# Four-layer hybrid model on one Trainium2 core: activations as the loaded operand, weights streamed 512 columns wide

## The chip, the cores and the metric

One program on one core of a Trainium2 chip. The metric is the time of one execution in microseconds of device time; lower is better. Three executions of the kernel before are listed, and one further execution was taken by the hardware profiler. The engines are named as the profile names them: PE is TensorE's matrix multiplications and PEld its loads of the stationary operand, DVE is VectorE, ACT is ScalarE, POOL is GpSimd, and SP is the engine whose queue issues most of the transfers.

## The reference: what is computed

256 tokens of 1024 features go through four layers. Each layer is a half-weighted SwiGLU feed-forward network (FFN), a mixer, and a second FFN, each on an RMS-normed input and added to the residual x. The mixers are S5, HGRN2, a gated delta net (GDN) and MoBA attention, one per layer. A last RMS norm gives the output.

```python
def _swiglu(x, w_gate, w_up, w_down):
    return (jax.nn.silu(x @ w_gate) * (x @ w_up)) @ w_down
...
    for i in range(DEPTH):
        m, j = i % N_MIXERS, i // N_MIXERS
        x = x + 0.5 * _swiglu(_rms(x, norm_g[i, 0]), ffn_w_gate[i, 0], ffn_w_up[i, 0], ffn_w_down[i, 0])
        h = _rms(x, norm_g[i, 1])
...
        x = x + y.astype(x.dtype)
        x = x + 0.5 * _swiglu(_rms(x, norm_g[i, 2]), ffn_w_gate[i, 1], ffn_w_up[i, 1], ffn_w_down[i, 1])
    return _rms(x, final_norm_g)
```

The inner width of an FFN is 2816, so an FFN multiplies by two matrices of 1024 x 2816 and one of 2816 x 1024, all in 32-bit floats. There are eight FFNs; they hold most of the weights.

## The kernel before, in words

Every product is split in three. A weight tile is cut into a high part (`hi`, a rounding copy on ScalarE, L73) and a low part (`lo`, the difference, on VectorE, L76), and the activations are cut likewise. `mm3` (L310 to L316) then issues high x high, high x low and low x high into one PSUM sum. All of them use the type float32r.

```python
        t.matmul(p, hi, ah, start=first, stop=False)
        t.matmul(p, hi, al, start=False, stop=False)
        t.matmul(p, lo, ah, start=False, stop=last)
```

The first operand of `matmul` is loaded into the array, 128 x 128, and the second streams through it. So in `mm3` the weights are loaded and the activations stream: x is kept turned, as `self.x` [128 features, 8, 256 tokens], with its split copies `self.xh` and `self.xl`, and a product streams 256 columns, the tokens. `col_tile` (L346) makes one tile of 128 output features x 256 tokens from 24 such products for 8 tiles of the contraction. Only `proj_rows` (L389, the v and gate projections of the mixers) loads x and streams weights, 256 columns wide (L400 to L402).

The class `Weights` plans all weights of the program in the order of use. A block is a transfer of up to 1 MB on SP's queue, four of them are held (`RAW`); a unit is 128 x 1024 elements, eight tiles of the contraction x 128 features, and four units are held in split form (`HL`). `take` hands out a unit and `pump` starts the loads and the splits that have become possible. Each unit feeds 24 products.

`ffn` (L414) goes over 22 tiles of the inner width. For each it makes the gate's and the up projection's tile, and `evac` (L420) makes the inner activations: a product with the norm's factors on VectorE (`a`), Silu on ScalarE (`sl`), a product with the up tile on VectorE (`h`), and the split (`hh` on ScalarE, `hl` on VectorE). The result already lies as the next products want it, with features on the partitions. `residual` (L452) makes the eight tiles of the down projection; each is scaled by the norm's factors (`part`), added to x and handed to `done_x` (L206), which splits it for the next part (`xh`, `xl`), squares it on ScalarE (`sq`) and sums the squares on GpSimd (`sqsum`). At the start of a part `norm_col` (L266) and `norm_due` (L275) make the norm's factors with small products on TensorE.

Beside the first FFN run the preparations of S5 (`s5_prep`, L602), spread over the FFN's steps. The bias table of MoBA (`moba_bias`, L1733) is asked for after the second FFN's inner loop; a DMA on ScalarE's queue copies it to DRAM (`bias_rows`, L1750). The order on each engine is not the order of the code: a scheduler places the instructions by its own estimate of when their operands are there, except where the code pins them. Within an engine the order is then fixed, and an instruction that waits holds all behind it.

## Time and profile before

| what | value |
|---|---|
| three executions, median (lowest to highest) | 2305.3 us (2305.07 to 2307.87) |
| the profiled execution: its span (no other time of it is listed) | 2303.2 us |
| TensorE products / weight loads | busy 2184.3 us (95%) / 2128.4 us (92%), 18575 each |
| VectorE, ScalarE, GpSimd | busy 1612.2 us (70%), 1152.3 us (50%), 362.7 us (16%) |
| DMA | 390.02 MB, mean 169 GB/s |

A busy TensorE is not one at its peak: the ends of its products are modelled and overlap, so its pace is read from the distance of one start to the next. A part's limit is read in its own stretch, since the eight FFNs and the four mixers have different ones.

### The profile page before, as it was taken

What the parts mean: (1) busy time and instruction counts of PE and PEld (TensorE: products, weight loads), DVE (VectorE), ACT (ScalarE), POOL (GpSimd) and SP (SyncE); (2) the same over time, 40 slices, a digit from 0 to 9 for tenths busy, and PEclk for the clock granted to TensorE, in tenths of its full rate; (3) what the DMA queues carried; (4) which work ended last, traced back from release to release, by engine and by line L of the source; (5) the groups of instructions that cost most, each with busy time, mean ns of one, the idle gap of its engine ahead of it and who ended that gap; (6) DMA issues with size and microseconds to landing.
All of it is one profiled execution on the core that took longest, in us unless ns stands there. A gap on an engine that the chain in (4) does not pass through costs nothing.

```text
span 2303.2 us, 44828 instructions
## 1 busy us (share of the span) xinstructions
PE 2184.3 (95%) x18575; PEld 2128.4 (92%) x18575; DVE 1612.2 (70%) x2712; ACT 1152.3 (50%) x1920; POOL 362.7 (16%) x380
## 2 busy tenths in 40 slices
PE   8979887999999999999999888889999999999998
PEld 7978677999999999999999777789999999999998
DVE  7998655666666877666667788877666666666664
ACT  5544334444445755444444476664544444455443
POOL 1499620001001000001001333222000000001001
PEclk9999888999999999999999999999999999999999
DMA  8656956655556535546555433224555555645553
GB/s 232 191 165 223 246 117 192 190 168 192 183 179 195 178 120 186 187 159 193 183 179 184 150 102 101 75 84 146 181 185 180 173 188 186 208 153 167 187 163 101
DMA packets 380572, 390.02 MB, mean 169 GB/s; under 512 B 11392, under 2 KB 374080, under 8 KB 379344
## 3 DMA queue, kind: packets, MB, share of 16 engines
q1 hardware_dynamic: 377520, 383.91, 53.1%
q10 hardware_dynamic: 2656, 3.16, 0.8%
q8 instruction: 145, 2.38, 0.4%
q0 software_dynamic: 192, 0.10, 0.1%
q14 instruction: 59, 0.48, 0.1%
HBM read 375.12 MB, written 12.01 MB: 168 GB/s over the span
## 4 chain that ended last, share of the span: by engine, by line
PE 78%; DVE 9%; ACT 3%; POOL 3%; DMA 3%; issue 3%; SPq 0%; ACTq 0%; DVEq 0%; POOLq 0%
PE acc L315 24%; PE acc L314 23%; PE acc L316 23%; DVE lo L76 2%; DMA tab<-s_k 1%; DVE cy L1422 1%; DMA raw<-in_s_w_glu_dram 1%; PE acc L401 1%; PE acc L400 1%; PE acc L402 1%; ACT hi L73 1%; DVE xl L221 0%; POOL s5e L742 0%; POOL s5e L743 0%; ACT zb L1546 0%
## 5 line engine op out<-in xcount | busy, mean ns | idle before, releaser
L76 DVE TENSOR_TENSOR lo<-raw,hi 128x1024 fp32r<-128x1024 f32 (+1 forms) x664 | 816.6, 1231 | 379.8 <-ACT hi L73 372.3
L73 ACT CAST hi<-raw 128x1024 fp32r<-128x1024 f32 (+1 forms) x697 | 714.6, 1028 | 665.9 <-PE acc L315 447.3
L315 PE MATMUL acc<-xl,hi 128*128 128x256 f32 x3336 | 946.8, 284 | 3.3 <-DVE xl L221 3.2
L314 PE MATMUL acc<-xh,hi 128*128 128x256 f32 x3336 | 946.6, 284 | 2.0 <-ACT xh L220 1.4
L316 PE MATMUL acc<-xh,lo 128*128 128x256 f32 x3336 | 944.6, 283 | 0.9 <-DVE lo L76 0.9
L315 PEld LDWEIGHTS acc<-xl,hi 128*128 128x128 f32 x3336 | 635.5, 191 | 6.1 <-DVE xl L221 5.3
L314 PEld LDWEIGHTS acc<-xh,hi 128*128 128x128 f32 x3336 | 634.7, 190 | 5.9 <-issue 2.3
L316 PEld LDWEIGHTS acc<-xh,lo 128*128 128x128 f32 x3336 | 635.0, 190 | 1.9 <-DVE lo L76 1.2
L314 PE MATMUL acc<-hh,hi 128*128 128x256 f32 x1408 | 401.1, 285 | 5.5 <-ACT hi L73 5.5
L316 PE MATMUL acc<-hh,lo 128*128 128x256 f32 x1408 | 400.1, 284 | 0.6 <-DVE lo L76 0.6
L315 PE MATMUL acc<-hl,hi 128*128 128x256 f32 x1408 | 400.2, 284 | 0.0
L314 PEld LDWEIGHTS acc<-hh,hi 128*128 128x128 f32 x1408 | 269.2, 191 | 6.3 <-ACT hi L73 5.7
L316 PEld LDWEIGHTS acc<-hh,lo 128*128 128x128 f32 x1408 | 268.6, 191 | 0.9 <-DVE lo L76 0.9
L315 PEld LDWEIGHTS acc<-hl,hi 128*128 128x128 f32 x1408 | 268.7, 191 | 0.4 <-issue 0.4
L238 POOL TENSOR_TENSOR sqsum<-sq 128x256 f32<-128x256 f32 x13 | 14.4, 1110 | 1120.7 <-ACT sq L230 1120.7
L427 ACT CAST hh<-h 128x256 fp32r<-128x256 f32 x176 | 71.1, 406 | 204.3 <-DVE h L426 204.1
L428 DVE TENSOR_TENSOR hl<-h,hh 128x256 fp32r<-128x256 f32 x176 | 77.5, 442 | 69.5 <-ACT hh L427 69.5
L422 DVE TENSOR_TENSOR a<-acc,r_row 128x256 f32<-128x256 f32 x176 | 74.4, 423 | 69.3 <-PE acc L316 69.1
L238 POOL TENSOR_TENSOR sqsum<-sqsum,sq 128x256 f32<-128x256 f32 x65 | 63.6, 978 | 304.5 <-ACT sq L230 292.4
L76 POOL TENSOR_TENSOR lo<-raw,hi 128x1024 fp32r<-128x1024 f32 x33 | 82.3, 2495 | 179.3 <-ACT hi L73 166.0
L424 ACT ACTIVATE sl<-a 128x256 f32<-128x256 f32 x176 | 72.6, 413 | 45.9 <-DVE a L422 45.6
L400 PE MATMUL acc<-hi,xh 128*128 128x256 f32 x320 | 93.2, 291 | 0.0
(576 smaller groups left out, 2669.6 us busy)
## 6 DMA issues: line engine op xcount, KB each, us to landing
raw<-in_ffn_w_gate_dram SPq DMA_DIRECT2D x87, 1024.0 KB, 5.4
raw<-in_ffn_w_up_dram SPq DMA_DIRECT2D x87, 1024.0 KB, 5.8
raw<-in_ffn_w_down_dram SPq DMA_DIRECT2D x64, 1024.0 KB, 5.4
raw<-in_ffn_w_down_dram SPq DMA_DIRECT2D x32, 768.0 KB, 4.7
raw<-in_gdn_w_in_dram SPq DMA_DIRECT2D x24, 1024.0 KB, 5.5
raw<-in_hg_w_in_dram SPq DMA_DIRECT2D x16, 1024.0 KB, 5.4
raw<-in_moba_w_in_dram SPq DMA_DIRECT2D x12, 1024.0 KB, 5.3
raw<-in_s_w_glu_dram SPq DMA_DIRECT2D x8, 1024.0 KB, 8.5
```

Source lines behind the costliest of these rows:

```text
L73: pin(self.nc.scalar.copy(hi, src))
L76: eng.tensor_tensor(lo, src, hi.bitcast(F32), op=OP.subtract)
L238: eng.tensor_tensor(s, self.sq[0], sq, op=OP.add)
L314: t.matmul(p, hi, ah, start=first, stop=False)
L315: t.matmul(p, hi, al, start=False, stop=False)
L316: t.matmul(p, lo, ah, start=False, stop=last)
L400: self.nc.tensor.matmul(p[:, t], xh, hi[:, k % 4], start=k == 0, stop=False)
L401: self.nc.tensor.matmul(p[:, t], xl, hi[:, k % 4], start=False, stop=False)
L422: nc.vector.tensor_tensor(a, p[:, 0], self.r_row, op=OP.mult)
L424: nc.scalar.activation(sl, a, AF.Silu)
L427: nc.scalar.copy(hh[:, f], h)
L428: return nc.vector.tensor_tensor(hl[:, f], h, hh[:, f].bitcast(F32), op=OP.subtract)
```

## The change

The two operands change places in nearly all products. The activations become the loaded operand, 128 features x 128 tokens, and the weights stream, 512 columns wide; one product now does the work of two. x lies as rows of tokens, `self.x` [128 tokens, 2, 1024]. A unit of weights is now two tiles of the contraction x 512 columns, and feeds twelve products (`Model.wide`): three for each tile of the contraction and each half of the tokens. For the FFN's inner layer the 512 columns are 256 of the gate and 256 of the up matrix, brought by two transfers into one block. The q and k projections and the like (`proj_cols`) stay as they were.

What follows from the turned layout:

- An output tile is now [128 tokens, 512 features], so the FFN's inner activations have to be turned before the down projection: `turn` transposes four tiles of 128 x 128 on TensorE per 256 inner features, one unit's products behind, and the split follows from PSUM in tiles of 128 x 512.
- The norm's factor is a scalar per partition and goes into Silu and into the last scale; the instructions `a` and `part` are gone.
- `turn_x` transposes each finished 128 x 512 piece of x on TensorE and splits it from PSUM. Squares are summed by ScalarE's accumulator; GpSimd's sums, and the small products of the norm on TensorE, go (they stay in the three mixers that still use the row `r_row`).
- The last units of a product (`tail`) are taken together, so that the first half of the tokens ends early and is turned while the second half is multiplied; the first product of a part starts with that first half.
- The final output needs no transposes.

```diff
-    def block(self, w, k0, nk, c0, ncol, units):
+    def wide(self, srcs, k0, nk, first=False):
+        step = 2 if first else 4
+        for k in range(k0, k0 + nk, step):
+            n = min(step, k0 + nk - k)
+            self.units += self.block(srcs, k, n, [(u, 2, 0, 512) for u in range(0, n, 2)])
...
+    def wide(self, p, unit, a, k, t, first, last):
+        hi, lo = unit
+        mm = self.nc.tensor.matmul
+        n = hi.shape[1]
+        for j in range(n):
+            ah, al = [a[:, k + j, m, t * 128:t * 128 + 128] for m in range(2)]
+            mm(p, ah, hi[:, j], start=first and j == 0, stop=False)
+            mm(p, ah, lo[:, j], start=False, stop=False)
+            mm(p, al, hi[:, j], start=False, stop=last and j == n - 1)
+
+    def product(self, a, n, done, tail=0, step=None, ps=None, k0=0, opens=True, closes=True):
+        if ps is None:
+            ps = [self.acc.tile([128, 512], F32, name="acc") for _ in range(2)]
+        u = 0
+        while u < n:
+            m = tail if n - u == tail else 1
+            units = self.w.take(m)
+            for t in range(2):
+                for j, unit in enumerate(units):
+                    self.wide(ps[t], unit, a, k0 + 2 * (u + j), t, opens and u + j == 0, closes and u + j == n - 1)
+                if u + m == n and done is not None:
+                    done(t, ps[t])
+            u += m
...
-            a = w.block(g, 0, KT, c, 256, [(0, KT, 0, 128), (0, KT, 128, 128)])
-            b = w.block(u, 0, KT, c, 256, [(0, KT, 0, 128), (0, KT, 128, 128)])
+            w.wide([(g, c, 256), (u, c, 256)], 0, KT, not w.blocks)
...
-            def evac(f, p):
-                a = two.tile([128, L], F32, name="a")
-                nc.vector.tensor_tensor(a, p[:, 0], self.r_row, op=OP.mult)
-                sl = two.tile([128, L], F32, name="sl")
-                nc.scalar.activation(sl, a, AF.Silu)
-                h = two.tile([128, L], F32, name="h")
-                nc.vector.tensor_tensor(h, p[:, 1], sl, op=OP.mult)
-                nc.scalar.copy(hh[:, f], h)
-                return nc.vector.tensor_tensor(hl[:, f], h, hh[:, f].bitcast(F32), op=OP.subtract)
+            def evac(j, t, p):
+                sl = two.tile([128, 256], F32, name="sl", bufs=1)
+                nc.scalar.activation(sl, p[:, :256], AF.Silu, scale=self.r_col[:, t:t + 1])
+                if t == 0:
+                    waiting.append((j, two.tile([128, 2, 256], F32, name="h", bufs=1)))
+                return nc.vector.tensor_tensor(waiting[-1][1][:, t], p[:, 256:], sl, op=OP.mult)
+            def turn():
+                j, h = waiting.pop(0)
+                q = self.aux.tile([128, 512], F32, name="aux")
+                for f in range(2):
+                    for t in range(2):
+                        c = f * 256 + t * 128
+                        nc.tensor.transpose(q[:, c:c + 128], h[:, t, f * 128:f * 128 + 128], self.ident)
+                q = q.rearrange("p (f c) -> p f c", f=2)
+                hh = hhl[:, 2 * j:2 * j + 2, 0]
+                nc.scalar.copy(hh, q)
+                return nc.vector.tensor_tensor(hhl[:, 2 * j:2 * j + 2, 1], q, hh.bitcast(F32), op=OP.subtract)
...
+    def turn_x(self, t, c):
+        q = self.aux.tile([128, 512], F32, name="aux")
+        for j in range(4):
+            k = 4 * c + j
+            nc.tensor.transpose(q[:, j * 128:j * 128 + 128], self.x[:, t, k * 128:k * 128 + 128], self.ident)
...
+                nc.scalar.activation(self.xh[:, k, tok], p, AF.Copy, scale=g)
+                nc.vector.scalar_tensor_tensor(self.xl[:, k, tok], p, g, self.xh[:, k, tok].bitcast(F32),
+                                               op0=OP.mult, op1=OP.subtract)
```

In the built programs 14784 products of 256 columns become 7392 of 512, and 1560 of 256 stay. The FFNs' inner layers add 352 transposes of 128 x 128, the turning of x adds 192, of which 16 replace those that turned the input before.

How the order moved, at three places. VectorE, near the end of a gate and up loop of an FFN; `hhl` is the split of the turned inner activations, `xhl` that of the turned x. Before:

```order
L76 TENSOR_TENSOR lo<-raw,hi 128x768
L422 TENSOR_TENSOR a<-acc,r_row 128x256
L76 TENSOR_TENSOR lo<-raw,hi 128x1024
L426 TENSOR_TENSOR h<-acc,sl 128x256
L428 TENSOR_TENSOR hl<-h,hh 128x256
```

and with the change:

```order
L430 TENSOR_TENSOR h<-acc,sl 128x256 x2
L91 TENSOR_TENSOR lo<-raw,hi 128x1024 x2
L443 TENSOR_TENSOR hhl<-aux,hhl 128x2x256
L91 TENSOR_TENSOR lo<-raw,hi 128x1024 x9
L484 SCALAR_TENSOR_TENSOR x<-acc,half,x 128x512 x2
L91 TENSOR_TENSOR lo<-raw,hi 128x1024
L241 SCALAR_TENSOR_TENSOR xhl<-aux,gains,xhl 128x128 x5
```

Both halves' `h` now stand ahead of the next two splits of weights, and the split of the turned activations comes two splits of weights later; `a` and the split without a transpose are gone.

TensorE, where one part's finished x meets the products around it. Before, at the start of an FFN's products, with the norm's small products between:

```order
L315 MATMUL acc<-xl,hi 128x256
L316 MATMUL acc<-xh,lo 128x256
L270 MATMUL aux<-mean_col,sqsum 128x1 x2
L314 MATMUL acc<-xh,hi 128x256
L315 MATMUL acc<-xl,hi 128x256
```

and with the change, in the middle of a down projection, with the transposes (L230) of both halves of x's first 512 features:

```order
L348 MATMUL acc<-lo,hhl 128x512
L230 MATMUL aux<-ident,x 128x128 x4
L349 MATMUL acc<-hi,hhl 128x512
L230 MATMUL aux<-ident,x 128x128 x4
L347 MATMUL acc<-hi,hhl 128x512
```

The transposes stand among the products, so any product behind them waits if x is late.

ScalarE, where MoBA's bias rows are copied out at the end of S5 (`part` is the gated linear unit of S5, `sl` the first Silu of the FFN behind it). Before:

```order
L1737 DMA tab<-in_rel_bias_table_dram 8x32x1
L982 CAST yh_3636<-ysum 128x256
L73 CAST hi<-raw 128x1024
L1750 DMA bias_rows<-row 1024x1x384
L73 CAST hi<-raw 128x1024 x3
L1034 ACTIVATE part<-acc 128x256 x2
```

and with the change:

```order
L1706 DMA tab<-in_rel_bias_table_dram 8x32x1
L240 ACTIVATE xhl<-aux,gains 128x128 x2
L246 ACTIVATE junk,ssq<-x 128x512
L240 ACTIVATE xhl<-aux,gains 128x128
L1719 DMA bias_rows<-row 1024x1x384
L240 ACTIVATE xhl<-aux,gains 128x128
L427 ACT_TABLE_LOAD
L427 ACTIVATE sl<-acc,norm_r 128x256
```

The copy moved from ahead of the gated linear unit to behind it, into the last splits of x for the following FFN.

## Rows read from the trace of the kernel before

**Rows 1.** The page, busy time and share of the span by engine.
```profile
PE 2184.3 (95%) x18575; PEld 2128.4 (92%) x18575; DVE 1612.2 (70%) x2712; ACT 1152.3 (50%) x1920; POOL 362.7 (16%) x380
```

**Rows 2.** The page, the chain that ended last, by engine.
```profile
PE 78%; DVE 9%; ACT 3%; POOL 3%; DMA 3%; issue 3%; SPq 0%; ACTq 0%; DVEq 0%; POOLq 0%
```

**Rows 3.** Stretches: length, busy PE, PEld, DVE, ACT, POOL (count), PEclk, DMA share, GB/s.
```profile
563.70:753.20 189.50, 189.47 (x1595) 188.99 (x1594) 123.28 (x186) 91.45 (x131) 8.73 (x14) 1.00 0.58 186
60.00:230.00 170.00, 153.14 (x1312) 149.22 (x1311) 158.23 (x209) 74.57 (x116) 129.68 (x115) 0.95 0.59 191
257.00:375.00 118.00, 89.63 (x996) 76.86 (x995) 73.77 (x115) 38.86 (x71) 43.24 (x96) 0.81 0.74 173
1271.60:1612.80 341.20, 296.65 (x2572) 269.10 (x2571) 279.07 (x592) 210.14 (x464) 100.64 (x52) 0.96 0.34 106
363.00:366.00 3.00, 3.00 (x16) 3.00 (x16) 2.96 (x5) 2.13 (x5) 0.12 (x1) 0.50 0.60 199
```

**Rows 4.** What TensorE waited for: us in total, times, longest us.
```profile
PE acc L314 <- ACT hi L73: 18.8, 4, 12.5
PE aux L755 <- DVE s5e L749: 16.5, 7, 3.7
```

**Rows 5.** Timeline of PE in S5's gated linear unit: start us, busy us, instruction.
```profile
361.51 0.42 PE L314 MATMUL acc<-yh,hi 128*128 128x256 f32 x1
...
365.13 0.42 PE L316 MATMUL acc<-yh,lo 128*128 128x256 f32 x1
```

**Rows 6.** Timeline of PE in MoBA's v projection, activations loaded, weights streaming.
```profile
2071.11 0.28 PE L401 MATMUL acc<-hi,xl 128*128 128x256 f32 x1
...
2074.83 0.28 PE L402 MATMUL acc<-lo,xh 128*128 128x256 f32 x1
```

**Rows 7.** Timeline of PE, plain 32-bit products of 256 columns, two together.
```profile
2075.59 0.60 PE L1806 MATMUL aux<-pT,v 128*128 128x256 f32 x2
```

**Rows 8.** Groups by line and shape, PE: count, busy us, mean ns.
```profile
L1806 PE MATMUL aux<-pT,v 128*128 128x256 f32 x16 | 4.9, 386 | 0.0
```

**Rows 9.** Timeline of PE, three transposes between products of 256 columns.
```profile
2054.27 0.28 PE L402 MATMUL acc<-lo,xh 128*128 128x256 f32 x1
2054.39 0.27 PE L1796 MATMUL aux<-ident,e 128*128 128x128 f32 x1
...
2054.61 0.27 PE L1798 MATMUL aux<-ident,e 128*128 128x128 f32 x1
2054.64 0.37 PE L400 MATMUL acc<-hi,xh 128*128 128x256 f32 x1
2054.84 0.28 PE L401 MATMUL acc<-hi,xl 128*128 128x256 f32 x1
```

**Rows 10.** Groups by line and shape, DVE and ACT: count, busy us, mean ns.
```profile
L76 DVE TENSOR_TENSOR lo<-raw,hi 128x1024 fp32r<-128x1024 f32 x600 | 753.0, 1256 | 309.7 <-ACT hi L73 302.2
L426 DVE TENSOR_TENSOR h<-acc,sl 128x256 f32<-128x256 f32 x176 | 73.5, 418 | 2.6 <-ACT sl L424 2.5
L1685 DVE SCALAR_TENSOR_TENSOR go<-aux,gd_w,go 128x512 fp32r<-128x512 f32 x8 | 5.9, 749 | 2.5 <-ACT go L1684 2.3
L73 ACT CAST hi<-raw 128x1024 fp32r<-128x1024 f32 x633 | 661.5, 1048 | 569.9 <-PE acc L315 353.4 <-issue 150.9 <-PE acc L401 26.2
```

**Rows 11.** Timeline of ACT and its queue around MoBA's bias rows, in S5.
```profile
317.38 0.29 ACTq L1737 DMA_DIRECT2D tab<-in_rel_bias_table_dram  x1
...
324.53 0.80 ACTq L1750 DMA_DIRECT2D bias_rows<-row  x1
...
358.77 1.04 ACT L73 CAST hi<-raw 128x1024 fp32r<-128x1024 f32 x1 [21.49 <-DMA raw<-in_s_w_glu_dram]
```

**Rows 12.** Transfers issued from 290 to 376 us: count, KB each, median us to landing.
```profile
raw<-in_s_w_glu_dram SPq DMA_DIRECT2D x3, 1024.0 KB, 30.8
```

**Rows 13.** Timeline of the kernel's end.
```profile
2291.98 0.28 PE L316 MATMUL acc<-hh,lo 128*128 128x256 f32 x1
...
2297.70 0.93 ACTq L307 DMA_DIRECT2D out_dram<-x_out  x2
```

More of the change, by code (lines that the diff above doesn't have):

```diff
@@ L105, in __init__ @@
             getattr(self, "plan_" + p[0])(*p[1:])
-        with tc.tile_pool(name="first", bufs=1) as pool, self.banks():
-            self.start(pool.tile([128, 2, D], F32, name="x_in"))
+        with self.banks():
+            self.start()
         self.prep = self.ahead = None
@@ L125, in __init__ @@
                 aux.enter_context(self.banks(1 if p[0] == "gdn" else 4))
[L126 to L131 removed]
+                self.due = p[0] in ("hgrn", "gdn", "moba")
+                if p[0] != "s5":
+                    self.r_col = self.norm_col()
                 if p[0] == "s5":
@@ L134, in __init__ @@
                     self.prep = None
[L135 to L141 removed]
                 if nxt is None:
[L143 removed]
+                    self.end = aux.enter_context(self.tc.tile_pool(name="last", bufs=1))
+                    self.fin = self.end.tile([128, D], F32, name="fin")
+                    nc.scalar.dma_start(self.fin, as_ap(I["final_norm_g"], 0, [[0, 128], [1, D]]))
+                getattr(self, p[0])(*p[1:])
                 aux.close()
@@ L336, in settle @@
                 self.beside.remove(g)
+    def wide(self, p, unit, a, k, t, first, last):
[20 more added lines that the diff above has]
+            u += m
+            for _ in range(m):
+                self.tick()
+                if step is not None:
+                    step()
+        return ps
     def col_tile(self, p, ah, al):
@@ new lines, in ffn, with step @@
+            steps = [0]
+            def step():
+                steps[0] += 1
+                n = steps[0]
+                if n % 4 == 1 and waiting and n > 4:
+                    turn()
+                if self.prep is not None and n > 4:
+                    for _ in range(n % 2 if n < 32 else 1 if n < 60 else 0):
+                        next(self.prep, None)
+            for j in range(FT // 2):
+                self.product(self.xhl, KT // 2, lambda t, p: evac(j, t, p), tail=0 if j else 4, step=step)
@@ L445, in ffn, with late @@
                 self.bias = None
-            if self.ahead is not None:
-                with self.tc.issue_after(done.ins):
+            ahead = self.ahead
+            def late():
+                step()
+                if not waiting and self.ahead is not None:
                     self.ahead()
-                self.ahead = None
-            self.residual(hh, hl, 0.5, scaled=True)
-    def residual(self, hh, hl, factor, scaled, done=True):
+                    self.ahead = None
+            self.residual(hhl, half, late)
@@ L503, in plan_s5, with done @@
+        n = a.shape[1] // 2
+        for c in range(2):
+            def done(t, p):
+                x = self.x[:, t, c * 512:c * 512 + 512]
+                if factor is None:
+                    nc.vector.tensor_tensor(x, p, x, op=OP.add)
+                else:
+                    nc.vector.scalar_tensor_tensor(x, p, factor[:, t:t + 1], x, op0=OP.mult, op1=OP.add)
+                self.done_x(t, c)
+            self.product(a, n, done, tail=min(4, n) if c else 0, step=step)
     def plan_s5(self, i):
@@ L1006, in gelus @@
                         low(half, j + n, two[n])
+            yhl = []
+            for half in range(2):
+                tags.append(tags.pop(0))
+                yhl.append(self.s5_pool.tile([128, 4, 2, L], F32R, name=f"yhl{half}", tag=tags[-1]))
             gelus(0)
-            held = self.w.take(4)
-            ahead = []
-            for k in range(2):
-                p = self.acc.tile([128, 2, L], F32, name="acc")
-                pin(mm(p.rearrange("p a c -> p (a c)"), self.zero[:, :128], self.zero, start=True, stop=False))
-                for n in range(2):
-                    half_tile(p[:, n], held[2 * k + n], 0, False, False)
-                ahead.append(p)
+            ahead = self.product(yhl[0], 2, None, closes=False)
@@ L1041, in plan_hgrn @@
+            for j in range(4):
+                if j:
+                    ahead = self.product(yhl[0], 2, None, closes=False)
+                self.product(yhl[1], 2, lambda t, p: glu(j, t, p), tail=2 if j == 3 else 0, ps=ahead, opens=False)
     def plan_hgrn(self, i):
@@ L1669, in turn @@
             def turn(z):
-                z.ohl = [two.tile([128, 4, L], F32R, name=f"go{n}") for n in range(2)]
+                z.ohl = two.tile([128, 4, 2, L], F32R, name="go")
                 o, ms = z.o, z.ms
```

459 lines of the change are left out of this document (167 added, 292 removed).

## The prediction

> **What bounds the kernel now.** I read the page first, then the chain that ended last, then stretches by stage, and last the timeline of TensorE. The page has TensorE busy 95% of the span, and its weight loads 92% [rows 1]; the chain lies on TensorE for 78% [rows 2]. That is an average over stages, so the stretches matter. In a clean FFN, from 563.70 to 753.20, TensorE is busy for 189.47 of 189.50 us, VectorE for 123, and the 16 DMA engines for 0.58 of the time: TensorE alone sets the pace there [rows 3]. Its 1595 instructions take 0.1188 us each. Three stages are different: in the first FFN, VectorE is busy for 158 of 170 us with S5's preparations beside it; S5 itself leaves TensorE idle for a quarter of 118 us; GDN leaves it idle for 45 of 341 us [rows 3]. What TensorE waits for longest are one split of a weight unit, 12.5 us in S5, and VectorE's preparations in the first FFN [rows 4].
>
> The question is then what sets 0.119 us for a product of 256 columns. Two rows decide it. Late in S5 the granted clock is 0.50, which is 1.2 GHz [rows 3], and there the same products start 3.62 / 17 = 0.213 us apart [rows 5]. That is one column per cycle at 1.2 GHz with nothing on top: 256 / 1.2. At 2.4 GHz the columns alone would then take 0.107, and the other 0.012 us is something that does not grow with the columns and that is hidden when the columns take 0.213. The load of the 128 x 128 operand is the candidate: transposes, with as large a load and little else, start 0.11 us apart [rows 9]. So at full clock the load and not the stream sets the pace, and a stream of 512 columns, 0.213 us at 2.4 GHz, should hide it as the half-clock one does. Plain 32-bit products support this at full clock: two together are busy 0.60 us and one alone 0.386, so they start 0.214 apart although each loads its own operand [rows 7, 8]. Which operand is loaded doesn't matter by itself: the v projection, which loads the activations already, runs at 3.72 / 31 = 0.120 [rows 6].
>
> **The change, part by part.** Durations come from the profiled execution, whose span is 2303.2 us; the median of the runs is 2305.3, 2.1 more.
>
> *Products.* 14784 of 256 columns become 7392 of 512. Two before took 2 x 0.1188 = 0.2376 us. One after takes at least 0.213 [rows 5] and at most 0.2376, if nothing is hidden. I take 0.216, since the row it is nearest to is the pair at 0.214 [rows 7, 8]. That saves 7392 x 0.0216 = 160 us; the ends are 182 and 0.
>
> *Transposes.* 352 + 192 - 16 = 528 are added. Three between products stretch two steps of products from 0.24 to 0.57 us [rows 9], so one costs 0.11, and all cost 58 us. The cost lies wholly on TensorE's path.
>
> Each is busy for 0.27 us in the rows, but the starts are 0.11 apart, so most of that overlaps with the next one [rows 9]; not overlapped, the 528 would cost 143 us. The Trainium skill, TensorE: Matmul & The Clock Gate, section "Part 4: PE-mode transpose", speaks against the change here: it puts a transpose of 128 x 128 at about 275 ns in a kernel, most of it access latency. The trace agrees in the duration and not in the spacing; by 275 ns each the 528 would cost 145 us (an estimate from that page).
>
> *Small products that go.* 44 recorded for the norm's sums, 32 of the 44 for its row, and 16 transposes of the final x, each about a transpose: 92 x 0.11 = 10 us back. Sum so far: -160 + 58 - 10 = -112.
>
> *Evacuation.* VectorE does, per 256 inner features, four splits of weights at 1.256, two `h` at 0.418 and one turned split at about 0.75 (the nearest row is a split from PSUM of 128 x 512): 6.6 us [rows 10]. TensorE takes 48 x 0.216 + 4 x 0.11 = 10.8 us for the same. ScalarE, with four copies at 1.048, is below VectorE. So neither becomes the bound, and the cover for these instructions is twelve products, 2.6 us, between the end of a block and its transposes. `h` stands ahead of the next splits on VectorE, so it is there about 1.1 us after the last product. I cost these waits at 5 us in all, 0.04 for each of 132 groups of transposes; the bounds are 0 and, if each group waits for half a weight split on VectorE, 132 x 0.63 = 83 us.
>
> *The part's end.* x's last half is updated, turned, split and squared while the next part multiplies the first half's 24 products, 24 x 0.216 = 5.2 us. Where the next part is an FFN nothing shows; I cost it at 0. At the kernel's end there are 5.7 us from the last large product to the output's transfers [rows 13]; the new end has no transposes: -2, between 0 and -3.
>
> *S5 and the bias rows.* The copy of MoBA's bias rows is issued at 324.53, and the weight transfers that meet it take 30.8 us to land; ScalarE waits 21.49 us for one, and TensorE 12.5 of it and then runs at half clock [rows 4, 11, 12]. That is some 15 us with the slow clock. With the change the copy stands behind the gated linear unit, so this stall goes. But it now meets the first loads of the following FFN, which needs 1 MB every 5.2 us and starts with at most six such blocks in hand, about 31 us of work. I give back half: -15 + 7 = -8, between -15 and +5. Between the bias table's load and the copy ScalarE's queue was held for 7.1 us [rows 11]; the last splits of x now stand behind that copy, and TensorE has 5.2 us of first-half products against it: +2, between 0 and +7.
>
> *Stages that TensorE does not bound.* In GDN 384 and in the first FFN 792 wide products save less than their 8 and 17 us, since other waits follow: +6, between 0 and +14.
>
> *Moved transfers.* SP issues more transfers (two for each gate and up block), but the bytes are the same, and the DMA engines are at 0.58 in a clean FFN; at the new pace that is 0.62. I cost it at 0, covered by four blocks of prefetch; without this cover it is the case above.
>
> Sum: -112 + 5 - 2 - 8 + 2 + 6 = -109, so a span of 2194, and 2196 as a median of runs.
>
> **The rivals.**
>
> *The stream itself is slow at full clock.* If float32r columns arrive no faster than 256 in 0.1188 us whatever the clock would allow, a product of 512 takes 0.2376, the first term is 0 and the transposes stay: 2196 + 160 = 2356, slower. For it: full clock has no row of such a product at 0.107. Against it: it would be a chance that load and stream lie so close. It decides from 0.216 + 109 / 7392 = 0.231 us for a product on. Chance 0.08.
>
> *A fixed gap of 0.012 stays on each product.* Then 0.2255, and 7392 x 0.0095 = 70 us less: 2266. The half-clock rows show no such gap, and the pair at 0.214 shows none. 0.06.
>
> *The transposes wait for VectorE.* Half a split for each group gives 2196 + 78 = 2274; the order on VectorE, with `h` first, speaks against it, the turned x in the down projection, three products behind the update, for it. 0.10.
>
> *The transposes cost their full latency.* Among streams that need the array for 0.213 each they might not overlap as they do in the rows. At 0.27 instead of 0.11, 528 x 0.16 = 84 us: 2280. The starts 0.11 apart speak against it [rows 9]. 0.03. The Trainium skill's section named above has this price.
>
> *The rest gains too.* VectorE is relieved in the first FFN and GDN (`a`, `part` and half of `hl`'s count go), the bias copy hides, nothing waits: without +5, +6, +7, +2 and with some 10 us from VectorE-bound stretches, 2166. 0.12.
>
> **How the numbers follow.** The forecast, 2196 with 2175 to 2225 by its own unknowns, has 0.61. The range from 2155 to 2283 takes in the rivals at 2166, 2266, 2274 and 2280 and leaves out the slow stream and the upper tail of the waits. A measurement of this kernel tells about 0.2% from no change. Faster by more than that: all but the slow stream and a little of the waits' tail, 0.90. Within 0.2%: that little, 0.02. Slower: 0.08.
>
> **What would show it.** In the new profile, large products of 512 columns start 0.213 to 0.220 us apart; at 0.23 or more the load was not the limit and the forecast falls. A clean FFN takes 792 x 0.216 + 60 x 0.11 = 178 us where 189.5 stood. Transposes appear in groups of four that stretch the stream by about 0.44 us; longer stretches, with VectorE as releaser, mean the third rival. TensorE's wait for S5's weights is gone from the top of its waits, and if it came back in the next FFN, a wait for the gate's or up's transfers is there. The transfers' share in a clean FFN is near 0.62.

## The result and the profile after

The changed kernel takes 2291.39 us (median of 5 runs, 2289.63 to 2291.76); the kernel before took 2307.87 beside it (2305.07 to 2313.03). The ratio is 0.9932, with an interval of 0.9914 to 0.9951. So the change is faster by some 0.7%: 16.5 us between these medians, and 13.4 between the spans of the two profiled executions. 109 us was forecast, and 2291 lies outside the range of 2155 to 2283. The profiled execution took 2291.63 us, its span is 2289.8.

The page of the changed kernel, busy time by engine, and the chain that ended last, by engine:

```profile
PE 2177.5 (95%) x11480; PEld 1774.8 (78%) x11480; DVE 1460.9 (64%) x2412; ACT 1159.5 (51%) x1876; POOL 286.8 (13%) x305
...
PE 81%; DVE 9%; ACT 3%; DMA 3%; POOL 2%; issue 1%; SPq 0%; ACTq 0%; DVEq 0%; POOLq 0%
```

Against [rows 1], TensorE has 7095 recorded instructions less and is busy for nearly as long: 2177.5 against 2184.3 us. The weight loads fell from 92% to 78% of the span, and VectorE by 151 us, but the chain still lies on TensorE [rows 2]. What the change relieved was not what set the pace.

Stretches of the changed kernel (length, busy PE, PEld, DVE, ACT, POOL with counts, PEclk, DMA share, GB/s): the first FFN, S5, the FFN after S5, the next FFN, and GDN.

```profile
9.81:247.20 237.39, 219.10 (x1075) 171.89 (x1076) 184.87 (x304) 115.54 (x175) 134.22 (x134) 0.96 0.69 219
247.20:350.09 102.89, 78.88 (x688) 58.91 (x687) 72.47 (x122) 39.51 (x76) 34.11 (x63) 0.90 0.78 173
350.09:552.90 202.81, 193.59 (x853) 156.14 (x852) 105.24 (x136) 92.62 (x128) 4.83 (x27) 0.97 0.60 176
552.90:745.09 192.19, 192.19 (x855) 154.85 (x853) 106.77 (x149) 92.65 (x126) 3.27 (x8) 1.00 0.56 181
1268.92:1604.52 335.60, 294.04 (x2196) 242.96 (x2195) 275.59 (x574) 208.62 (x461) 98.75 (x48) 0.97 0.36 112
```

The clean FFN of [rows 3], the fourth line, was to fall from 189.5 to 178 us. It takes 192.2, with TensorE busy for all of it. By the same cuts, at the first product of each part, the stages moved like this (the same cuts before: 248.8, 116.0, 189.0, 189.6 and 341.2 us for these five):

| stage | before | after | difference |
|---|---|---|---|
| first FFN | 248.8 | 237.4 | -11.4 |
| S5 | 116.0 | 102.9 | -13.1 |
| FFN after S5 | 189.0 | 202.8 | +13.9 |
| the five other FFNs up to MoBA, HGRN and MoBA together | | | +7.8 |
| GDN | 341.2 | 335.6 | -5.6 |
| last FFN and the end | 202.4 | 197.6 | -4.8 |

The first FFN and GDN, where VectorE has a large share, and the end gained a little. The stages that TensorE sets, which were to give nearly all of it, gave nothing. S5's gain came back in the FFN behind it.

The first FFN before, by the same cut, and TensorE's waits in it that bear on this, before and after:

```profile
9.93:258.70 248.77, 222.24 (x1883) 215.96 (x1883) 213.32 (x357) 117.63 (x183) 148.58 (x152) 0.95 0.66 207
```

```profile
PE acc L314 <- ACT hi L73: 6.1, 2, 5.5
```

```profile
PE aux L760 <- POOL s5e L734: 11.8, 6, 3.5
PE aux L746 <- DVE s5e L740: 4.2, 2, 2.9
```

TensorE's idle time there fell from 26.5 to 18.3 us. The waits for S5's preparations hardly changed: 16.9 us before [rows 4], with 0.4 for GpSimd, and 16.0 after. The 6.1 us of waits for a split of weights went.

**The products.** TensorE in the clean FFN, start and busy us: gate and up products, with one group of four transposes at the front, then down products of the same FFN.

```profile
602.19 0.39 PE L349 MATMUL acc<-hi,xhl 128*128 128x512 f32 x1
602.42 0.60 PE L439 MATMUL aux<-ident,h 128*128 128x128 f32 x4
602.77 0.48 PE L347 MATMUL acc<-hi,xhl 128*128 128x512 f32 x1
603.09 0.40 PE L348 MATMUL acc<-lo,xhl 128*128 128x512 f32 x1
...
613.87 0.39 PE L349 MATMUL acc<-hi,xhl 128*128 128x512 f32 x1
...
695.71 0.39 PE L348 MATMUL acc<-lo,hhl 128*128 128x512 f32 x1
...
703.41 0.40 PE L348 MATMUL acc<-lo,hhl 128*128 128x512 f32 x1
```

From 603.09 to 613.87 are 46 steps of 0.2343 us; from 695.71 to 703.41 are 33 steps of 0.2333. 0.216 was forecast. The two steps of products around the transposes take 0.90 us instead of 0.47: 0.43 for four transposes, as forecast. The same down products in a later FFN:

```profile
1751.80 0.39 PE L349 MATMUL acc<-hi,hhl 128*128 128x512 f32 x1
...
1756.79 0.39 PE L347 MATMUL acc<-hi,hhl 128*128 128x512 f32 x1
```

Here 22 steps take 4.99 us, 0.2268 each, and these starts are perfectly even (0.226 and 0.227 in turn). So there are two spacings at the full clock, 227 and 233 to 234 ns, with the same instruction, shapes and engines around it. Of the 7392 products, xhl's 4704, the down products of three FFNs and HGRN's 96 have the longer one; the down products of five FFNs (1320) and 480 others the shorter or nearly so (227 to 230 on the mean). The products thus take some 5592 x 0.2342 + 1800 x 0.2269 = 1718 us; the 14784 before took 1756. The gain of the wide stream is 38 us, where 160 were forecast.

And one more stretch, behind a wait of TensorE, where the granted clock is 0.50 (from 394 to 400 us):

```profile
396.46 0.63 PE L347 MATMUL acc<-hi,xhl 128*128 128x512 f32 x1
...
399.87 0.63 PE L349 MATMUL acc<-hi,xhl 128*128 128x512 f32 x1
```

Eight steps in 3.41 us are 0.426 each, 512 columns at 1.2 GHz and nothing on top, like [rows 5]. At 2.4 GHz the columns alone would take 0.213, so here too something of 13 to 21 ns is on top at the full clock alone, and the length of the product didn't hide it.

**S5's stall.** What was waited for from 330 to 420 us in the changed kernel (us in total, times, longest us):

```profile
DVE lo L91 <- ACT hi L88: 36.1, 20, 17.5
ACT hi L88 <- DMA raw<-in_ffn_w_up_dram: 18.1, 2, 17.6
PE acc L347 <- ACT hi L88: 8.5, 1, 8.5
```

The wait of [rows 4] and [rows 11] is gone from S5 and stands, with 17.6 us on ScalarE and 8.5 on TensorE, in the FFN behind it. The stretch in which the copy of the bias rows runs beside the weights (columns as above):

```profile
358.00:390.00 32.00, 27.43 (x121) 21.31 (x119) 12.51 (x16) 12.04 (x17) 0.00 (x0) 1.00 0.59 92
```

The DMA engines are as busy as in the whole FFN, 0.59 of the time, but move 92 GB/s where the FFN's mean is 176.

### The profile page after: what moved, and what is told of

The parts are those of the page before. It is cut to its first block, busy times and chain, and to the rows that moved or that the text cites. A ratio compares the mean times of both kernels' runs of the same rounds, so it can differ in the third digit from the quotient of the medians.

```text
span 2289.8 us, 30309 instructions
## 1 busy us (share of the span) xinstructions
PE 2177.5 (95%) x11480; PEld 1774.8 (78%) x11480; DVE 1460.9 (64%) x2412; ACT 1159.5 (51%) x1876; POOL 286.8 (13%) x305
## 4 chain that ended last, share of the span: by engine, by line
PE 81%; DVE 9%; ACT 3%; DMA 3%; POOL 2%; issue 1%; SPq 0%; ACTq 0%; DVEq 0%; POOLq 0%
PE acc L348 23%; PE acc L349 23%; PE acc L347 23%; DVE lo L91 2%; PE acc L316 2%; PE acc L315 2%; PE acc L317 2%; PE aux L439 2%; DVE cy L1395 1%; DMA raw<-in_ffn_w_up_dram 1%; ACT hi L88 1%; PE aux L230 1%; DMA tab<-s_k 1%; POOL s5e L734 1%; POOL s5e L733 1%
## 5 line engine op out<-in xcount | busy, mean ns | idle before, releaser
L91 DVE TENSOR_TENSOR lo<-raw,hi 128x1024 fp32r<-128x1024 f32 x648 | 809.8, 1251 | 614.1 <-ACT hi L88 613.1
L88 ACT CAST hi<-raw 128x1024 fp32r<-128x1024 f32 x681 | 712.5, 1048 | 734.2 <-PE acc L349 680.9
L347 PE MATMUL acc<-hi,xhl 128*128 128x512 f32 x1568 | 635.0, 405 | 10.4 <-ACT hi L88 9.6
L348 PE MATMUL acc<-lo,xhl 128*128 128x512 f32 x1568 | 627.9, 400 | 2.4 <-DVE lo L91 2.3
L349 PE MATMUL acc<-hi,xhl 128*128 128x512 f32 x1568 | 626.4, 400 | 0.0
L347 PEld LDWEIGHTS acc<-hi,xhl 128*128 128x128 f32 x1568 | 298.2, 190 | 81.0 <-ACT hi L88 10.5
L349 PEld LDWEIGHTS acc<-hi,xhl 128*128 128x128 f32 x1568 | 297.9, 190 | 73.9 <-issue 2.7
L348 PEld LDWEIGHTS acc<-lo,xhl 128*128 128x128 f32 x1568 | 298.2, 190 | 72.4 <-DVE lo L91 4.9
L349 PE MATMUL acc<-hi,hhl 128*128 128x512 f32 x704 | 278.0, 395 | 0.0
L347 PE MATMUL acc<-hi,hhl 128*128 128x512 f32 x704 | 277.9, 395 | 0.0
L348 PE MATMUL acc<-lo,hhl 128*128 128x512 f32 x704 | 277.0, 393 | 0.0
L347 PEld LDWEIGHTS acc<-hi,hhl 128*128 128x128 f32 x704 | 132.9, 189 | 28.8
L349 PEld LDWEIGHTS acc<-hi,hhl 128*128 128x128 f32 x704 | 132.8, 189 | 28.7
L316 PE MATMUL acc<-xhl,hi 128*128 128x256 f32 x520 | 148.8, 288 | 0.3 <-DVE xhl L241 0.3
L315 PE MATMUL acc<-xhl,hi 128*128 128x256 f32 x520 | 148.9, 289 | 0.1
```

The source lines that it names most:

```text
L88: pin(self.nc.scalar.copy(hi, src))
L91: eng.tensor_tensor(lo, src, hi.bitcast(F32), op=OP.subtract)
L347: mm(p, ah, hi[:, j], start=first and j == 0, stop=False)
L348: mm(p, ah, lo[:, j], start=False, stop=False)
L349: mm(p, al, hi[:, j], start=False, stop=last and j == n - 1)
```

## The experiments

What needed explaining was the spacing. Theory A: a fixed time for each product, and a penalty for where the two operands lie in memory. The tiles' addresses suggested it: the weights' parts begin at 83936 bytes of a partition. One hhl tile with the short spacing begins at 116704, a multiple of 64 bytes from them; xhl, with the long one, begins at 27712, which is not. The rivals: B, a stream that is slow for each column; C, a slowdown by the other engines or the transfers.

**1. Products alone.** The only work is runs of products, for example:

```diff
+    for name, n, c, m, w in CONFIGS:
...
+        for i in range(N):
+            a = w // 4 + i % 12 * 128
+            s = m // 4 + i % 4 * 512 if n < 512 else m // 4 + i % 3 * 512
+            pin(nc.tensor.matmul(p[:c, :n], loaded[:, a:a + c], streamed[:, s:s + n], start=i == 0, stop=i == N - 1))
...
```

> The model is left out: the program holds only runs of 42 products in a row, one run for each case, and its output is not the reference's. In the trace of the changed kernel the products of 512 columns start 227 ns apart where the loaded activations and the streamed weights both begin 32 bytes into a 64-byte line (hhl at 116704, hi at 83936), and 234 ns apart where one begins at 0 and the other at 32 (xhl at 27712); in the kernel before it is 120.0 and 117 to 119 ns for 256 columns. Theory A (a fixed time for each product, and besides it a penalty of where the two operands lie towards each other): equal places give 120 ns at 256 columns, 173 at 384, 227 at 512 and 67 at 128, both at 0 as well as both at 32; unequal places give 234 at 512 and 117 to 119 at 256; fewer loaded columns shorten the fixed time in proportion if it is the load's. Theory B (the stream of float32r has a rate of 0.44 to 0.46 ns a column): 512 columns cost twice 256 wherever the operands lie, 234 to 240. Theory C (the other engines or the transfers slow the array): alone, with VectorE, ScalarE and the queues idle, all cases of 512 columns start 216 ns apart, as the bf16 products of zeros do in the changed kernel.

The two tiles lie 8448 bytes apart, 33 times 256; places are called alike where both operands have the same offset from there. Measured: 512 float32r columns go at 226.7 ns with both operands at 32, and with both at 0 after nine products at 224 to 236; they go at 232 to 234 with a difference of 4, 16, 32, 48, 64, 96 or 128 bytes (230.6 at 8). 384 columns take 173.3, 256 take 120.0 (alike) and 117 to 118 (not), 128 take 110 to 112. Two more cases, the same operand loaded for every product and two sums taken in turn, keep 226.7 too, so neither a new operand nor the adding into one sum is what costs. Two stretches of this run, bf16 products of 512 columns (41 steps) and plain 32-bit products of 256 columns (42 products leave 84 records, two passes each; 82 steps):

```profile
215.92:224.78 8.86, 8.86 (x44) 4.03 (x42) 0.18 (x1) 0.00 (x0) 0.00 (x0) 1.00 0.00 0
224.99:242.70 17.71, 17.71 (x84) 15.59 (x83) 0.19 (x1) 0.00 (x0) 0.00 (x0) 1.00 0.00 1
```

That is 216 ns a step for both. C falls: with the other engines idle the float32r products keep their 227 and 233. B falls for like places: 512 columns cost 107 ns more than 256 there, which is 256 columns at 2.4 GHz, and the rest, 13.3 ns, is the same at 256, 384 and 512. For unlike places it holds nearly: 117 to 118 at 256 and 233 at 512 look like a rate. What A had wrong is the multiple: a difference of 64 or 128 bytes isn't alike. Loading 64 or 32 columns instead of 128 left 230 to 239, so the extra time isn't a share of the load's length.

The Trainium skill, TensorE: Matmul & The Clock Gate, section "Back-to-back issue gap", gives N / 2.4 + 2.5 ns as the isolated gap of a product of N columns, 216 for 512, and about 131 for 512 columns in a stream of loads and products. The bf16 run, a stream with a load for each product, agrees with the 216, and no run here comes near 131. Float32r takes 11 to 18 ns more than the 216; a pass of the plain 32-bit product takes 216 too, but for only 256 columns.

**2. 32 bytes ahead of the weights.**

```diff
+        pad = ctx.enter_context(tc.tile_pool(name="pad", bufs=1))
+        nc.vector.memset(pad.tile([128, 8], F32, name="pad"), 0.0)
         raw = ctx.enter_context(tc.tile_pool(name="raw", bufs=Weights.RAW))
```

> The changed kernel with 32 bytes left free ahead of the weights' tiles, so that the weights' parts begin at 0 of a 64-byte line instead of 32, and everything allocated behind them moves with them (hhl too); xhl stays where it is, at 0. If what counts is whether the two operands lie alike (A), the gate and up products and the other projections of xhl go from 234 to 227 ns, the down products keep what they have (227 in five FFNs, 234 in three, since hhl and the weights move together): about 4200 + 576 + 192 products by 7.4 ns, 35 us less than the changed kernel, some 2256 us. If it is the place of the loaded operand alone (A2), xhl stays at 234, the down products of five FFNs go from 227 to 234 (+10 us) and those of three from 234 to 227 (-6 us): some 2295 us. If the spacing has nothing to do with addresses (B, C): 2291 us.

Measured: 2278.56 us (2276.85 to 2284.36). xhl's products went from 234.1 to 233.4 ns and not to 227; the down products of three FFNs kept 233 to 234, those of five kept 227. So neither A with its 64 bytes nor A2 held: weights and hhl moved together and nothing changed for them, which speaks for the distance between the two, but a distance of 192 modulo 256 is no better than 160. 0.7 ns on xhl's products is 3 us; the other 10, some 7 of them in S5 and the FFN behind it, no run explains.

**3. The width alone.** The roles stay, the stream is cut in two:

```diff
-            mm(p, ah, hi[:, j], start=first and j == 0, stop=False)
-            mm(p, ah, lo[:, j], start=False, stop=False)
-            mm(p, al, hi[:, j], start=False, stop=last and j == n - 1)
+            for n0, (act, w) in enumerate(((ah, hi), (ah, lo), (al, hi))):
+                opens, closes = first and j == 0 and n0 == 0, last and j == n - 1 and n0 == 2
+                for c in ((0, 512),) if opens or closes else ((0, 256), (256, 512)):
+                    mm(p[:, slice(*c)], act, w[:, j, slice(*c)], start=opens, stop=closes)
```

> The changed kernel with every streamed product of 512 columns cut into two of 256, except the first and the last of each group: the roles of the operands stay swapped, only the width goes back. Theory A: pairs of 256 cost 240 ns where 512 cost 227, and 234 to 238 where 512 cost 234: 13 ns for some 2000 pairs and 0 to 4 for some 5000, so 25 to 45 us more than the changed kernel, 2317 to 2336 us. Theory B: no change, 2291 us. The prediction's price (0.2376 against 0.216 us) would make it 150 us more, 2440 us.

Measured: 2339.33 us (2336.95 to 2339.59), 48 more than the changed kernel and 1.3% slower than the kernel before (1.0130, 1.0100 to 1.0159). So the width of nearly all products is worth 48 us and not 160, a little over the upper end for A, and the swap without it would lose. The prediction's price is out by a factor of three.

**4. One transpose instead of four.**

```diff
-                for f in range(2):
-                    for t in range(2):
-                        c = f * 256 + t * 128
-                        nc.tensor.transpose(q[:, c:c + 128], h[:, t, f * 128:f * 128 + 128], self.ident)
+                nc.tensor.transpose(q[:, :128], h[:, 1, 128:], self.ident)
+                q = q[:, None, :128].to_broadcast([128, 4, 128])
...
```

> The changed kernel with one transpose instead of four in each turn of the FFN's inner layer (its copies read that one block four times, so three quarters of h are left out of the result): 264 transposes less. If each is worth the 0.11 us between two starts, 29 us less than the changed kernel, 2262 us. If the copies on ScalarE and VectorE behind the transposes are what the products wait for, or the time of a transpose is hidden beside the products, under 5 us.

Measured: 2265.99 us (2261.84 to 2268.67), 25.4 less: 0.096 for each of 264 transposes. In the clean FFN it is 188.60 us instead of 192.19, 0.109 for each of 33. So they lie on TensorE's path at close to their spacing of 0.11, and 528 cost 51 to 58 us. The copies behind them stayed and the time went, so the products don't wait for those.

**5. Which distance.**

```diff
+    (512, 0, 32), (512, 0, 64), (512, 0, 128), (512, 0, 160), (512, 0, 0), (512, 0, 256), (512, 96, 96), (512, 96, 0),
+    (256, 0, 0), (256, 0, 32), (256, 0, 128), (384, 0, 0), (384, 0, 160))]
...
```

> The model is left out again: runs of 150 float32r products each, the two tiles 8448 bytes (33 x 256) apart, shifted by the bytes in the name. In the run of products alone, 512 columns were 226.7 ns apart for equal shifts and 232 to 234 for every other difference, 64 and 128 bytes among them, though a run of equal shifts began with six products at 231 to 235. Moving the weights by 32 bytes, to a distance of 192 modulo 256 from xhl, left xhl's products at 233. Theory A256 (the spacing is fixed, columns + 32 at 2.4 GHz, where the operands lie a multiple of 256 bytes apart, and otherwise about 1.09 of the columns): differences 0, 256 and 96/96 give 226.7; 32, 64, 128, 160 and 96/0 give 233.3; 256 columns give 120.0 at 0 and 117 to 118 at 32 and 128; 384 give 173.3 at both. Theory A-lock (the array falls into the fixed spacing after some products whatever the difference): long runs at 64 or 128 end at 226.7 as well. In the run with four transposes every 48 products, the products go back to 226.7 within some six.

Measured, stretches of 149 steps each, in the order of the list (columns, offset of the streamed tile, offset of the loaded one); the last two are 256 columns at 0/0 and 0/32:

```profile
15.83:50.78 34.95, 34.95 (x152) 28.15 (x150) 0.00 (x0) 0.00 (x0) 0.00 (x0) 1.00 0.00 1
51.01:85.78 34.77, 34.77 (x151) 28.01 (x150) 0.19 (x1) 0.00 (x0) 0.00 (x0) 1.00 0.00 0
86.00:120.63 34.63, 34.63 (x151) 28.07 (x149) 0.19 (x1) 0.00 (x0) 0.00 (x0) 1.00 0.00 0
120.86:155.63 34.77, 34.77 (x150) 27.97 (x149) 0.19 (x1) 0.00 (x0) 0.00 (x0) 1.00 0.00 0
155.86:189.68 33.82, 33.82 (x150) 27.96 (x149) 0.19 (x1) 0.00 (x0) 0.00 (x0) 1.00 0.00 0
189.91:223.68 33.77, 33.77 (x150) 27.96 (x149) 0.19 (x1) 0.00 (x0) 0.00 (x0) 1.00 0.00 0
223.91:257.73 33.82, 33.82 (x150) 27.97 (x149) 0.19 (x1) 0.00 (x0) 0.00 (x0) 1.00 0.00 1
257.97:292.74 34.77, 34.77 (x151) 27.97 (x150) 0.19 (x1) 0.00 (x0) 0.00 (x0) 1.00 0.00 0
292.97:310.83 17.86, 17.86 (x150) 17.86 (x149) 0.19 (x1) 0.00 (x0) 0.00 (x0) 1.00 0.00 1
310.95:328.58 17.63, 17.63 (x151) 17.63 (x150) 0.19 (x1) 0.00 (x0) 0.00 (x0) 1.00 0.00 1
```

34.77 / 149 is 233.4 ns and 33.77 / 149 is 226.6. A256 holds: 0, 256 and 96/96 have the short spacing, 32, 64, 128 (232.4), 160 and 96/0 the long one to the end of the run. At 256 columns it is the other way round, 119.9 and 118.3. That would explain why it was not seen before: the two spacings differ by 1 to 3% there, with the sign against, and the 0.1188 of the prediction lies between them. After four transposes the even spacing is back after six to ten products. One miss: 384 columns in unlike places took 176.7 at a distance of 160, not 173.3.

**6. All operands in like places.**

```diff
+        nc.vector.memset(pad.tile([128, 24], F32, name="pad"), 0.0)
...
-            hhl = pool.tile([128, FT, 2, L], F32R, name="hhl")
+            n = FT * 2 * L
+            at = {(0, 0): 24, (1, 0): 8, (2, 0): 40}.get((i, s), 0)
+            hhl = pool.tile([128, n + 64], F32R, name="hhl")[:, at:at + n].rearrange("p (f m l) -> p f m l", f=FT, m=2)
...
```

> The changed kernel with 96 bytes left free ahead of the weights' tiles, so that xhl and the weights' parts lie a multiple of 256 bytes apart (27712 and 84032), and with hhl of the FFNs 00, 10 and 20 and the two o tiles of the HGRN part shifted by 32 to 160 bytes so that they do too. Theory A256: the products of xhl (4224 in the FFNs, some hundred elsewhere), 792 down products and 96 of the HGRN part go from 233 to 234 down to 227: some 5200 by 7 ns, 36 us less than the changed kernel, about 2255 us. If the difference has to be zero in some larger unit, or the writes of the other engines keep the products from the even spacing, part of it only: 2265 to 2291 us.

Measured: 2259.23 us (2256.73 to 2260.95), 32 less than the changed kernel; 0.9796 of before (0.9774 to 0.9817). The clean FFN, and its gate and up products:

```profile
545.32:732.39 187.07, 187.07 (x854) 154.55 (x853) 106.69 (x148) 92.58 (x126) 3.25 (x8) 1.00 0.57 186
```

```profile
607.10 0.39 PE L351 MATMUL acc<-hi,xhl 128*128 128x512 f32 x1
...
611.86 0.39 PE L351 MATMUL acc<-hi,xhl 128*128 128x512 f32 x1
```

21 steps in 4.76 us, 0.2267. The FFN loses 5.1 of 192.2 us, with every instruction the same. The effect of the operands' places is shown, by its sign, its size and its products. Experiment 2, which moved the tiles without making them alike, is the control: its spacings stayed within 1 ns.

**7. The bias rows in eight pieces.**

```diff
-        nc.scalar.dma_start(self.bias_rows, row.rearrange("h (o s) -> h o s", o=1).to_broadcast([8, 128, 384]))
+        self.rows_left = [(row, o) for o in range(0, 128, 16)]
...
+                if (i, s) == (0, 1):
+                    if n == 4:
+                        self.bias(pool)
+                    elif n > 4 and n % 4 == 3 and self.rows_left:
+                        self.bias_piece()
...
```

> The changed kernel with the copy of the bias rows (1.5 MB from 8 partitions) cut into eight pieces, one every four steps of the FFN that follows the S5 part, instead of one transfer at that FFN's end of gate and up. If the weights' transfers wait behind this one transfer, the single wait of 17.6 us of ScalarE's split for raw goes, and with it the 8.9 us in which TensorE has no product and the half clock behind it (3 us): 10 to 13 us less than the changed kernel, 2279 to 2282 us. If the copy's time is needed in any case because its packets go over the same engines: under 3 us.

Measured: 2278.10 us (2275.18 to 2280.47), 13.3 less. The FFN behind S5:

```profile
348.16:538.19 190.03, 190.03 (x854) 154.05 (x852) 104.89 (x136) 90.92 (x128) 4.82 (x27) 1.00 0.62 187
```

It takes 190.0 instead of 202.8 us, TensorE waits for nothing in it, and the transfers' share rose from 0.60 to 0.62: the same bytes went beside the weights. So the stall came from the copy as it stood, one transfer at one time. The edit changes the size of the transfers and their times together; which of the two counts was not tried apart.

**8. Both.**

> The two edits together, the places of the operands and the copy in pieces. If they are independent: 36 + 12 us less than the changed kernel, about 2243 us; by the bounds of the two, 2250 to 2280 us if the first gives only a part.

Measured: 2247.42 us (2247.13 to 2248.29), 44 less than the changed kernel, where the two alone gave 32 and 13. It is 0.9746 of before (0.9725 to 0.9767), the fastest of all and faster than both kernels.

**9. Which read.** What the extra time is was still open. Even means that the two operands lie a multiple of 256 bytes apart, odd that they lie 32 bytes off it.

```diff
+            act = loaded[:k, a:a + 128] if "onew" not in name else loaded[:k, a:a + 1].to_broadcast([k, 128])
+            w = streamed[:k, s:s + 512] if st == 1 else streamed[:k, s:s + 1024:2] if st == 2 else streamed[:k, s:s + 1].to_broadcast([k, 512])
...
```

> The model is left out: runs of 80 float32r products of 512 columns, with the operands a multiple of 256 bytes apart (even) or 32 bytes off it (odd). What is open is where the time beyond the columns (213.3 ns at full clock) comes from: 13.3 ns with even places, 20 with odd ones, none at half the clock. If it is the reading of the streamed operand from the memory that collides with the reading of the loaded one, then a stream that reads one column 512 times (one), or a load that reads one column 128 times (onew), comes down to about 216, and a stream of every second column (two) may cost more. If it is the passage of the loaded operand into the array, nothing of the streamed columns matters: all even cases stay at 226.7, and those with 64 or 32 partitions too; a load of fewer partitions changes neither.

Measured, 79 steps each: even, odd; one column streamed 512 times, even and odd; every second column; one column loaded 128 times, even and odd; then the run of 32 partitions, odd.

```profile
15.68:33.82 18.14, 18.14 (x81) 15.00 (x80) 0.00 (x0) 0.00 (x0) 0.00 (x0) 1.00 0.00 1
34.06:52.48 18.42, 18.42 (x80) 14.84 (x79) 0.19 (x1) 0.00 (x0) 0.00 (x0) 1.00 0.00 1
52.72:69.76 17.04, 17.04 (x80) 14.93 (x79) 0.19 (x1) 0.00 (x0) 0.00 (x0) 1.00 0.00 0
69.98:87.03 17.05, 17.05 (x80) 14.93 (x79) 0.19 (x1) 0.00 (x0) 0.00 (x0) 1.00 0.00 1
87.25:123.05 35.80, 35.80 (x80) 16.38 (x79) 0.19 (x1) 0.00 (x0) 0.00 (x0) 1.00 0.00 0
159.77:178.05 18.28, 18.28 (x80) 14.86 (x79) 0.19 (x1) 0.00 (x0) 0.00 (x0) 1.00 0.00 1
178.29:196.55 18.26, 18.26 (x81) 14.85 (x80) 0.19 (x1) 0.00 (x0) 0.00 (x0) 1.00 0.00 0
283.20:316.90 33.70, 33.70 (x80) 25.67 (x79) 0.19 (x1) 0.00 (x0) 0.00 (x0) 0.50 0.00 0
```

A stream that reads one column over and over goes at 17.04 / 79 = 215.7 ns, in both places, although each product loads its 128 x 128 operand as before. So the extra 11 to 18 ns hang on the reading of different streamed columns; the load as such costs nothing at this width. With a load that reads a single column the products take 231 ns in even and odd places alike (18.28 and 18.26 us): the extra stays, where about 216 was expected, and only the difference between the places goes. So that difference needs a load that reads different columns as well. With 64 partitions the spacings settle at 226.7 and 233 as with 128. What collides at the memory was not settled. The first even stretch began with slow products; its last 30 are at 226.7.

The Trainium skill, TensorE: Matmul & The Clock Gate, section "Step-by-step: what each phase is for", says that the load has a read port of its own and takes nothing from the running product's reading. For float32r the runs differ from that in one point: the spacing depends on how the loaded and the streamed operand lie towards each other, 227 or 233.

## Why the prediction was wrong

**The failed step** is in the first part of the prediction: "So at full clock the load and not the stream sets the pace, and a stream of 512 columns, 0.213 us at 2.4 GHz, should hide it as the half-clock one does." The reading that the extra 0.012 us at full clock doesn't grow with the columns was nearly right (13.3 ns at 256, 384 and 512 in like places). That it is the load, and that a longer product hides it, was the mistake. Experiment 9 has the same load under a product of 512 columns and no extra, 215.7 ns, where the stream reads one column over and over; with different columns it is 227 or 233. [Rows 5] show a product that is longer in time and at half the clock; the prediction took the first for the cause, and it was the second. The changed kernel has a product as long as that one, 0.213 us of columns with the same load, at the full clock, and the extra is there; at half the clock a product of 0.426 has none. The support was of another kind as well: the pair in [rows 7] and the mean in [rows 8] are plain 32-bit products. By experiment 1 such a product leaves two records, so the pair is most likely the two passes of one product; a pass takes 216 here too, as does a bf16 product of 512 columns. None of the rows was a float32r product whose columns took 0.213 at the full clock.

That the kernel became faster, to which the prediction gave 0.90, is luck as far as its mechanism goes: the products gave 38 us and the transposes took 51 to 57. What made it faster were the small products that went, and the first FFN, GDN and the end, with some 20 us.

**The sum by its terms.**

- Products: -160 forecast, -38 measured. Of the 122 us that are missing, 7392 x 0.0107 = 79 are the extra time that stays on every product in the best case, and some 43 the unlike places of xhl, three hhl tiles and HGRN's o tiles and what lies between; experiment 6 gave 32 us back.
- Transposes: +58 forecast, 51 (experiment 4) to 57 (0.43 for a group of four). Right; their full latency isn't paid, and that rival falls.
- Small products that go: -10 forecast. The trace has none of the 44 for the norm's sums left, 12 of the 44 for its row, and none of the final x's 16 transposes; no run prices them apart.
- Evacuation: +5 forecast. In the clean FFN 528 x 0.2342 + 264 x 0.2333 + 60 x 0.11 make 191.9 of its 192.19 us, which leaves next to nothing for a wait for `h` or its turned copies. The rival of transposes waiting for VectorE falls with it.
- S5 and the bias rows: -8 forecast. S5 lost 13.1 us and the next FFN gained 13.9, 12.8 of them the stall that experiment 7 takes away, so the term was about nothing. That the copy would meet the following FFN's first loads was seen; half of the stall was given back, and it was all of it. The +2 for splits of x behind the copy measured 0.2: TensorE's only wait for them in that FFN.
- Stages not bound by TensorE: +6 forecast as a loss against the products' price. Since that price shrank, the term can't be compared. The first FFN gave 11.4 us and GDN 5.6, as the last rival had it for stretches bound by VectorE; that VectorE's relief is the cause isn't shown. In the first FFN the waits for S5's preparations stayed at 16 us, and GDN's time moves by up to 3.9 us between the changed kernel and those of experiments 6 to 8 (339.5 us in experiment 6).
- The end: -2 forecast, -4.8 with the last FFN.
- Transfers: at no cost, as forecast; the share in a clean FFN is 0.56 and not 0.62, since the FFN didn't get shorter.

**The rivals.** The fixed gap that stays on each product (2266 us, chance 0.06) was the nearest, and too rarely believed: at the full clock the gap stays, whatever the width. Its 0.2255 is close to the 0.2267 measured for like places, so its time fits the kernel of experiment 6, which took 2259, and not the changed kernel, where most places are unlike. The slow stream was to decide from 0.231 us for a product on; the products came to 0.2324 on the mean, and yet the kernel is faster by 0.7%, because the first FFN, GDN and the end gave some 20 us. The mark that was named, "at 0.23 or more the load was not the limit and the forecast falls", was the right one to look at.

## What to carry to other kernels

Before a per-instruction time is split into a part that scales and a part that hides, find a row in which only one of the two quantities differs: here duration and clock changed together, and the type with the supporting row. Where every product of a kind is slower than its columns, compare the same instruction on tiles at different addresses; a few bytes of padding were worth 32 us, more than the 16 of the whole rewrite. And a transfer that stalls one stage is not gone when the change moves it: look at what it meets next, or cut it into pieces.

## What was not expected of the hardware

- For float32r, the distance between the streamed and the loaded operand modulo 256 bytes sets the spacing: 226.7 ns at 512 columns for a distance of 0, 231 to 234 for the others tried; at 256 columns 120.0 against 117 to 119. After a break the even spacing sets in after six to ten products.
- The extra time is absent at half the clock (0.426 us for 512 columns), for bf16 products (216 ns), and for a stream of one repeated column (216 ns).
- A stream of every second float32r column takes twice as long: 35.80 / 79 = 453 ns at a granted clock of 1.00.
- In the runs of 32 partitions TensorE was busy all the time and the granted clock still fell to 0.50, with 33.70 / 79 = 427 ns for a product; with 64 and 128 partitions it was 1.00. The runs of 32 stood last in one execution, and no other order was tried.
